# One more buffer for raw weights and for low halves, a byte mask for the scans, and reloads of gates, o, x and p at other products, in a fused short-convolution and gated-recurrence layer

## The chip, the core and the metric

The kernel runs on one core of one Trainium2 chip. The metric is the device time of one execution in microseconds (us). The core's engines appear in the profile as PE (TensorE's matmuls), PEld (its weight loads), DVE (VectorE), ACT (ScalarE), POOL (GpSimd) and SP (SyncE, here only an issuer of DMAs). DMAs are issued from two queues that matter here: SP's, which carries the weights, and POOL's, which carries activations to and from DRAM. Both are moved by the same 16 DMA engines.

## The reference, cut to what matters

One encoder layer on 2048 prompt tokens and 64 sample tokens, all in float32, with D_MODEL = 1024 and eight heads of 128:

```python
h = rms_norm(x, g_pre)
proj = jnp.einsum('btd,dn->btn', h, w_in)                 # 10 groups of 1024 columns
vA, bA, cA, zA, q, f, iv, zB, gA, gB = split_cols(proj)
u = cA * vA                                               # path a: a convolution over 3 tokens
yA = jnp.einsum('btc,cd->btd', jax.nn.silu(zA) * bA * causal_conv3(u_ext, conv_w), w_a_out)
fg = lb + (1.0 - lb) * jax.nn.sigmoid(f)                  # path b: a recurrence, head by head
S_new, o = hgrn2_scan(S0, silu(q) * QK_SCALE, 1.0 - fg, iv, jnp.log(fg))   # chunks of 64 tokens
o = o * lax.rsqrt(jnp.mean(o * o, axis=-1, keepdims=True) + EPS) * g_onorm
yB = jnp.einsum('btc,cd->btd', o * jax.nn.silu(zB), w_b_out)
merged = jax.nn.sigmoid(gA) * yA + jax.nn.sigmoid(gB) * yB
x = x + rms_norm(jnp.einsum('btd,de->bte', merged, w_o), g_post)
gate = jax.nn.sigmoid(jnp.einsum('btd,de->bte', rms_norm(x, g_ple), w_ple_gate))
x = x + jnp.einsum('btp,pd->btd', p, w_ple_proj) * gate
```

## The kernel before

**Blocks and halves.** The 2112 tokens are cut into three blocks of 768, 704 and 640 tokens. Activations lie with features on partitions; a tile of one feature block and all tokens of a block is an `r` tile (a ring of 50 of them), and a matmul takes half of the tokens: 384, 352 or 320 columns. To keep float32 accuracy with TensorE's fast form of it, each operand is split into a high half `hi` and a low half `lo`, and each product is three matmuls: hi by hi, hi by low activations, low weights by hi. The two lines of `split` (196) do it: ScalarE writes hi, VectorE subtracts it.

**Products.** The matrix products use a Strassen-like scheme with seven products instead of eight. A weight matrix is cut into 2 x 2 parts, and the parts or sums of parts (A11, A12, A22, S1 to S4) are the weights. A product here means the matmuls of one weight block of 128 x 512: 4 slices of K by 3, so 12 matmuls. A block's raw weights come by `load_raw` (line 206, 256 KB, tag `raw`, five buffers). For some, the low half is split on the spot into a `lo` tile; for the others it was stored in DRAM earlier (`low`) and is loaded again (line 228, 256 KB). `low_tile` says where a loaded low half goes: to tag `s` (three buffers) in turns 1, 3 and 5 of seven, else to `lo` (four buffers). `s` also holds the sums that the first block makes. There are five `hi` buffers. A DMA into a buffer can start when the last reader of the tile that had it before is done, and SP issues its DMAs strictly in order.

**Stages.** For each block: path b with the heads (and the gates' products between them, spilled to DRAM, line 777), path a (`path_a`), and then `in_turn` over three or four weight matrices: W_A (w_a_out), W_G (w_ple_gate, in the middle block only, and there for the rows of block 0), W_B (w_b_out), W_O (w_o). In `in_turn` each matrix has seven products n = 0 to 6 (A11, A12, S2, S3, A22, S1, S4), each for four g. So the products of a stage are numbered n x 4 + g: 20 is (W_A, n = 5, g = 0), 28 is (W_B, n = 0, g = 0). After these, the gates of the next block start (`gates`, by `sgroup`), and the norms of this block run between their first products.

**What is reloaded, and when.** `loads` is called after every product. The dict `plan` says which spilled tiles POOL reloads at which (matrix, n): gates GA and GB, o (the heads' outputs), h2 (block 0's normed rows for W_G). Such a reload is *paced*: it waits for the last matmul issued. `fetch` reloads the halves of x and p that W_G's sinks add (line 1163, two DMAs of 192 KB). `operands_in_steps` makes the operands of the next block, one step at each product in `STEPS_AT`; some steps load a pair of x (line 645, not paced). In the middle block products from 28 on are shifted by 28, since W_G stands between. `final_norm` loads x_fm (line 1205) for its residual: four at its start (three in the last block) and one with each j after that. POOL, too, issues in order.

**The scans.** `keep` is a mask of ones with a zero at each chunk's start; `tensor_tensor_scan` in `head_prep` (line 867) multiplies its running sum by it, once for each head and block.

Of the kernel before, what the change touches and what calls it, by code (L numbers as in the profile page):

```python
# [10 lines left out]
F32 = mybir.dt.float32  # L11
F32R = mybir.dt.float32r
I32 = mybir.dt.int32
AF = mybir.ActivationFunctionType
ALU = mybir.AluOpType
PSUM = bass.MemoryType.PSUM
# [25 lines left out]
LEAD = 7  # L42


STEPS_AT = (0, 8, 9, 10, 12, 13, 14, 15, 20)
STEPS_AT += (36, 37, 40, 41, 42, 43, 49, 53)
STEPS_AT += (57, 58, 65, 67, 68, 69, 70, 76)
STEPS_AT += (80, 81, 82, 83)


def plan():
# [37 lines left out]
def hybrid_step(  # L89
# [31 lines left out]
    def nm(s):  # L121
        uid[0] += 1
        return f"{s}_{uid[0]}"
# [27 lines left out]
    g_pre, g_on, g_post, g_ple = (vec[:, i, :] for i in range(4))  # L151
    cw = [vec[:, 4 + i, :] for i in range(3)]
    caus = const.tile([P, 2, P], I32, tag="caus", name="caus")
    keep = const.tile([P, MAXN], F32, tag="keep", name="keep")
    atts = [
        const.tile([P, max(len(b["parts"][i]) for b in blocks if i < len(b["parts"])), P], F32, tag=f"att{i}", name=f"att{i}") for i in range(NPART)
    ]
# [44 lines left out]


    def load_raw(src):
        raw = wp.tile([P, 4, P], F32, tag="raw", name=nm("raw"), bufs=5)
        SP.dma_start(raw, src)
        return raw

# [2 lines left out]
    def lo_tile():  # L211
        return wp.tile([P, 4, P], F32R, tag="lo", name=nm("lo"))

    def low_tile():

        turn[0] += 1
        return sum_tile(F32R) if turn[0] % 7 in (1, 3, 5) else lo_tile()

    def sum_tile(dt=F32):
        return wp.tile([P, 4, P], dt, tag="s", name=nm("s"), bufs=3)  # L220

    def split_w(raw, key=None, queue=SP, low=low_tile):

# [71 lines left out]
    def kept_w(i1, i2, name, anew=False, low=low_tile):  # L295

        keys = dict(A11=(i1, 0), A12=(i1, 1), A22=(i2, 1))
        if name in keys:
            return split_w(load_raw(w_blk[keys[name]]), None if anew else keys[name])
        return split_w(load_raw(sums[i1][name]), (i1, name), low=low)  # L300

    def combined(i1, i2, first):

        queue = SP if first else G
        with tc.high_priority():
            if not first and i1 in sums:
                lows_in = dict(S3=partial(sum_tile, F32R), S1=partial(sum_tile, F32R), S2=partial(sum_tile, F32R), S4=lo_tile)
                return {n: kept_w(i1, i2, n, True, lows_in.get(n)) for _, n, _, _, _ in PRODUCTS}
            a11, a21, a22, a12 = (load_raw(w_blk[i, h]) for i, h in ((i1, 0), (i2, 0), (i2, 1), (i1, 1)))
            out = dict(A11=split_w(a11))  # L310

            def total(name, x, y, op):
                s = sum_tile()
                V.tensor_tensor(s, x, y, op)
                out[name] = keep_sum(name, i1, s, queue) if first else split_w(s)
                return s

            total("S3", a11, a21, ALU.subtract)
            s1 = total("S1", a21, a22, ALU.add)
            s2 = total("S2", s1, a11, ALU.subtract)  # L320
            out["A12"] = split_w(a12)
            out["A22"] = split_w(a22)
            total("S4", a12, s2, ALU.subtract)
            return out
# [91 lines left out]
    def half(t, h):  # L416
        n = wide(t) // 2
        return t[:, h * n : (h + 1) * n]
# [207 lines left out]
    def rms(acc, out, segs, copy=A.copy):  # L626


        cols = col_rstds([acc[:, cols_of(sg)] for sg in segs], segs[0]["n"])
        yield  # L630
        for sg, col in zip(segs, cols):
            copy(out[:, cols_of(sg)], spread(col, sg["n"]))
        yield
# [448 lines left out]
    def ple(bl, ph, kept, held=None, shared=False):  # L1082


        for j in range(KB):
            if held is not None:
                hi, lo = held[j]
            else:
                raw = wp.tile([P, 4, P], F32, tag="raw", name=nm("raw"), bufs=5)[:, :2, :]
                SP.dma_start(raw, w_ple[j])  # L1090
                with tc.high_priority():
                    hi = wp.tile([P, 4, P], F32R, tag="hi", name=nm("hi"), bufs=5)[:, :2, :]
                    lo = low_tile()[:, :2, :]
                    A.copy(hi, raw)
                    SP.dma_start(lo.bitcast(F32), lows["p", j])
            t = rt(bl["n"])
            for s in bl["segs"]:
                pp, c = ps_attn()[:, : s["n"]], cols_of(s)
                for k, (xhi, xlo) in enumerate(ph):
                    T.matmul(pp, hi[:, k, :], xhi[:, c], start=k == 0, stop=False)  # L1100
                    T.matmul(pp, hi[:, k, :], xlo[:, c], start=False, stop=False)
                    last[0] = T.matmul(pp, lo[:, k, :], xhi[:, c], start=False, stop=k == 1).ins
                with tc.high_priority():
                    if shared and j < 4 and s is bl["segs"][1]:
                        V.tensor_copy(t[:, c], pp)
                    else:
                        copied = copies[0] = A.copy(t[:, c], pp).ins
            if bl["last"]:
                kept["p", j] = t
            else:  # L1110
                kept["p", j] = spill("p", j, wide(t))
                G.dma_start(kept["p", j], t)
                if not shared:
                    lows["p", j] = dram.tile([P, 2, P], F32, tag=f"lop{j}", name=nm("low"), bufs=1)
                    SP.dma_start(lows["p", j], lo.bitcast(F32))
            with behind_all((copied,) if hooks else ()):
                hook()
            yield
# [9 lines left out]
    def merge_in_turn(a, kept, mg, before):  # L1128

        ob, m = [], []  # L1130

        def gated(v, x, y):
            V.tensor_tensor(v, whole(x, y), v, ALU.mult)

        def sink_a(g, c, h, x, y):
            gated(half(m[g + c * KH], h), x, y)

        def sink_b(g, c, h, x, y):
            j = g + c * KH
            gated(half(mg[j], h), x, y)  # L1140
            V.tensor_tensor(half(mg[j], h), half(mg[j], h), half(m[j], h), ALU.add)

        plan = {
            (W_A, -1): (kept, GA, m),
            (W_A, 1): (kept, GA, m),
            (W_B, 1): (kept, GB, mg),
        }
        stages = [
            dict(idx=W_A, raw=a, sink=sink_a, anew=("A11", "A12")),
            dict(idx=W_B, raw=ob, sink=sink_b, anew=("A11", "A12")),  # L1150
        ]
        if before is None:
            plan |= {(W_A, 3): (kept, "o", ob), (W_A, 5): (kept, "o", ob), (W_A, 6): (kept, GB, mg)}
        else:
            rows, fetched = [], {}
            stages.insert(1, gate_in_turn(before[0], rows, lambda j, h: fetched.pop((j, h)), ("A11", "A12", "A22")))
            plan |= {(W_A, 3): (before[1], "h2", rows), (W_A, 5): (before[1], "h2", rows)}
            plan |= {(W_G, 1): (kept, "o", ob), (W_G, 2): (kept, "o", ob), (W_G, 6): (kept, GB, mg)}

        def fetch(j, h):  # L1160
            t = rt(before[0]["n"])
            for q, kind in enumerate("xp"):
                paced(G.dma_start(half(t, q), half(before[1][kind, j], h)))
            fetched[j, h] = half(t, 0), half(t, 1)

        def loads(idx, n, g=0, count=1):

            src, kind, tiles = plan.get((idx, n), (kept, None, m))
            if kind is not None:
                tiles.extend(reload(src[kind, j], n >= 0) for j in range(len(tiles), len(tiles) + count))  # L1170
            if idx == W_G and n in (0, 3, 4, 5):
                fetch(g + KH * (n in (3, 4)), int(n > 3))

        return stages, loads

# [17 lines left out]
    def final_norm(bl, segs, xo, acc, h2, kept, raw=False):  # L1193
# [10 lines left out]
                xks.append(rt(bl["n"]))  # L1204
                G.dma_start(xks[j][:, c], x_fm[j * P : (j + 1) * P, segs[0]["t0"] : segs[0]["t0"] + n])

        for _ in range(3 if bl["last"] else 4):
            fetch()
        copy = V.tensor_copy if bl["last"] else A.copy
        yield from rms(acc, rs, segs, copy)  # L1210
        for j in range(KB):
            fetch()
            xj = xo[j][:, c]
# [177 lines left out]
    for bi, bl in enumerate(blocks):  # L1391
# [14 lines left out]
        def side(rows, sums_):  # L1406
            for j in range(KB):
# [6 lines left out]
                    hooks.extend(partial(piece, sums_) if n in at else None for n in range(12))  # L1414
                yield

        def ready():
            a_first.extend(narrow(half(t, 0)) for t in a[:KH])

        path_a(bl, hc, a, first, side(rows, prepare_sums(in_path) if in_path else None), ready)  # L1420
        assert not hooks and (extra is None or next(extra, extra) is extra)
        mg, xo, h2, acc = [], [], [], []
        stages, loads = merge_in_turn(a, kept, mg, (blocks[0], kepts[0]) if middle else None)
        stages.append(out_in_turn(mg, xo, acc, ("A11", "A12", "A22") if bl["last"] else ()))
        if nxt:
            hc = new_operands()
# [5 lines left out]
        else:  # L1432
            rows2 = []
            again = rows_again(kepts[bi - 1], rows2)
        loads(W_A, -1, count=KH)
        for idx, n, g in in_turn(stages, a_first):
            loads(idx, n, g)
            if nxt:
# [75 lines left out]
```

## Time and profile before

| | |
|---|---|
| three runs, us | 2562.08, 2572.47, 2572.30 (median 2572.3) |
| the profiled execution's own time, us | 2571.89 |
| its span, first to last instruction, us | 2570.1 |
| granted TensorE clock, mean | 0.997 |
| DMA, mean over the span | 270 GB/s, 693.53 MB |

The profile's page has the span in 40 slices of 64 us, each digit a busy share in tenths:

```profile
PE   8999999999999999999999999999999999999999
DVE  8788888899989866677755577986566665568966
ACT  6666676554555666777845466666677754456736
POOL 1022121222110021223221013102100010011221
DMA  7677777898798797777777689989866667789977
```

A row of the waits is: engine, line, tile, what it waited for, us in total, times, the longest. A row of the windows is: start and end, length, then for each engine the busy time and the number of instructions, then granted clock, share of the DMA engines, GB/s. A row of the timeline is: start, length, engine, line, operation, out<-in, and in brackets the idle time before it with what ended it. In names, `raw`, `lo`, `s` and `hi` are tiles in the core's memory; `low`, `S` and `w_blk` are in DRAM.

### The profile page before, as it was taken

The page shows a single profiled execution, that of the slowest core. Times are in us where ns is not written, and L with a number is a line of the kernel's source. Part 1 is how long each engine was busy: PE and PEld are TensorE (multiplying, and loading weights), DVE is VectorE, ACT ScalarE, POOL GpSimd, SP SyncE. Part 2 cuts the span into 40 slices and gives each one's busy share as a digit, 9 for nine tenths or more (in the row PEclk, how much of TensorE's full clock was granted, in tenths as well). Part 3 has the DMA queues.
Part 4 walks back from the last instruction along what each step waited for, and adds up shares of the span by engine and source line. Part 5 has one row for each costly group of instructions (what it writes and reads, how often), then busy time and mean ns, then how long its engine had stood idle before and what let it go on. Part 6 is the DMA issues. An engine that isn't in the chain of part 4 may idle for free. (4 is left out here: it accounts for less than half of the span.)

```text
span 2570.1 us, 47304 instructions
## 1 busy us (share of the span) xinstructions
PE 2540.2 (99%) x16198; PEld 2525.4 (98%) x16198; DVE 1915.8 (75%) x3714; ACT 1617.3 (63%) x3136; POOL 421.0 (16%) x774
## 2 busy tenths in 40 slices
PE   8999999999999999999999999999999999999999
PEld 8999999999999999999999999999999999999998
DVE  8788888899989866677755577986566665568966
ACT  6666676554555666777845466666677754456736
POOL 1022121222110021223221013102100010011221
PEclk9999999999999999999999999999999999999999
DMA  7677777898798797777777689989866667789977
GB/s 269 211 262 276 275 249 265 295 317 304 264 323 265 243 342 259 257 261 267 253 263 231 215 304 358 331 276 330 308 202 198 196 207 236 233 281 337 312 263 256
DMA packets 330289, 693.53 MB, mean 270 GB/s; under 512 B 41632, under 2 KB 46272, under 8 KB 330048
## 3 DMA queue, kind: packets, MB, share of 16 engines
q1 hardware_dynamic: 283392, 513.73, 60.0%
q0 software_dynamic: 46368, 176.74, 19.0%
q8 instruction: 127, 2.08, 0.3%
q14 instruction: 114, 0.93, 0.1%
q10 hardware_dynamic: 288, 0.05, 0.0%
HBM read 507.10 MB, written 183.26 MB: 269 GB/s over the span
## 5 line engine op out<-in xcount | busy, mean ns | idle before, releaser
L385 PE MATMUL pg<-r,hi 128*128 128x320 f32 (+2 forms) x3304 | 1087.1, 329 | 0.0
L386 PE MATMUL pg<-r,hi 128*128 128x320 f32 (+2 forms) x3304 | 1067.8, 323 | 0.0
L387 PE MATMUL pg<-r,lo 128*128 128x384 f32 (+2 forms) x2368 | 771.6, 326 | 1.9 <-DMA lo<-low 1.9
L385 PEld LDWEIGHTS pg<-r,hi 128*128 128x128 f32 x3304 | 622.5, 188 | 0.4
L386 PEld LDWEIGHTS pg<-r,hi 128*128 128x128 f32 x3304 | 622.8, 188 | 0.0
L227 ACT CAST hi<-raw 128x512 fp32r<-128x512 f32 x544 | 335.2, 619 | 335.6 <-PE pg L386 131.6
L196 ACT CAST hi<-raw 128x512 fp32r<-128x512 f32 x454 | 280.9, 620 | 290.0 <-PE pg L386 133.4
L387 PEld LDWEIGHTS pg<-r,lo 128*128 128x128 f32 x2368 | 445.4, 188 | 2.4 <-DMA lo<-low 2.2
L196 DVE TENSOR_TENSOR lo<-raw,hi 128x512 fp32r<-128x512 f32 x454 | 311.6, 687 | 154.8 <-ACT hi L196 134.2
L520 PE MATMUL pg<-r,hi 128*128 128x384 f32 (+2 forms) x1232 | 398.7, 325 | 0.9 <-DVE r L196 0.7
L519 PE MATMUL pg<-r,hi 128*128 128x384 f32 (+2 forms) x1232 | 389.3, 326 | 0.4 <-ACT r L196 0.2
L387 PE MATMUL pg<-r,s 128*128 128x320 f32 (+1 forms) x936 | 296.6, 317 | 6.5 <-DMA s<-low 6.5
L196 DVE TENSOR_TENSOR r<-r,r 128x320 fp32r<-128x320 f32 (+6 forms) x426 | 245.9, 595 | 68.1 <-ACT r L196 66.1
L521 PE MATMUL pg<-r,lo 128*128 128x384 f32 (+2 forms) x860 | 278.5, 325 | 7.3 <-DMA lo<-low 7.3
L520 PEld LDWEIGHTS pg<-r,hi 128*128 128x128 f32 x1232 | 232.4, 189 | 4.6 <-DVE r L196 3.7
L196 ACT CAST r<-r 128x320 fp32r<-128x320 f32 (+6 forms) x426 | 221.0, 548 | 24.9 <-DVE r L366 16.2
L519 PEld LDWEIGHTS pg<-r,hi 128*128 128x128 f32 x1232 | 229.6, 189 | 4.9 <-ACT r L196 4.3
L387 PEld LDWEIGHTS pg<-r,s 128*128 128x128 f32 x936 | 176.8, 189 | 7.1 <-DMA s<-low 7.1
L196 ACT CAST hi<-s 128x512 fp32r<-128x512 f32 x160 | 98.7, 618 | 117.1 <-PE pg L386 104.0
L521 PEld LDWEIGHTS pg<-r,lo 128*128 128x128 f32 x860 | 161.9, 188 | 8.9 <-DMA lo<-low 8.9
L399 ACT COPY hf<-pg 128x352 f32<-128x352 f32 (+2 forms) x354 | 156.0, 444 | 10.4 <-PE pg L387 10.2
L432 DVE TENSOR_TENSOR r<-hf,pg 128x352 f32<-128x352 f32 (+2 forms) x118 | 60.9, 516 | 97.6 <-PE pg L387 97.6
(370 smaller groups left out, 3767.5 us busy)
## 6 DMA issues: line engine op xcount, KB each, us to landing
raw<-w_blk SPq DMA_DIRECT2D x550, 256.0 KB, 4.1
raw<-S SPq DMA_DIRECT2D x488, 256.0 KB, 3.8
s<-low SPq DMA_DIRECT2D x334, 256.0 KB, 4.0
lo<-low SPq DMA_DIRECT2D x210, 256.0 KB, 4.5
low<-lo SPq DMA_DIRECT2D x178, 256.0 KB, 3.0
S<-s SPq DMA_DIRECT2D x152, 256.0 KB, 3.2
low<-r POOLq DMA_DIRECT2D x88, 256.0 KB, 4.4
r<-w_blk POOLq DMA_DIRECT2D x72, 256.0 KB, 6.6
```

What stands on the lines that cost most here:

```text
L196: return A.copy(hi, src).ins, V.tensor_tensor(lo, src, hi.bitcast(F32), ALU.subtract).ins
L227: A.copy(hi, raw)
L385: add(hi[:, k, :], xhi, start=start and k == 0, stop=False)
L386: add(hi[:, k, :], xlo, start=False, stop=False)
L387: last[0] = add(lo[:, k, :], xhi, start=False, stop=k == KH - 1).ins
L399: copied = A.copy(got[n], ps[bank])
L432: V.tensor_tensor(dst, x, y, ALU.add)
L519: add(hi[:, k, :], xhi, start=start and k == 0, stop=False)
L520: add(hi[:, k, :], xlo, start=False, stop=False)
L521: last[0] = add(lo[:, k, :], xhi, start=False, stop=k == KH - 1).ins
```

## The change

- Raw weights have six buffers instead of five, `s` four instead of three. Loaded low halves go to `s` and `lo` by turns; in the groups whose sums are stored already (`combined`), S4's goes to `s` too, as those of S1, S2 and S3 did.
- `keep` is a tile of bytes, 768 bytes on each partition instead of 3072.
- In `STEPS_AT`, product 20 becomes 28: the load of the second pair of x for the next block's operands.
- In the middle block, o is reloaded at (W_A, 4) and (W_A, 6) instead of (W_G, 1) and (W_G, 2), and the 16 fetches of x and p stand at the products of `FETCH_AT` instead of all products of n = 0, 3, 4, 5.
- The first four gates GA are asked for ahead of path a's last group (`ready`), not behind it.
- `final_norm` asks for one x at its start and one after each of its steps, where it asked for four (three) together.

```diff
+FETCH_AT = (0, 1, 2, 3, 8, 9, 11, 12, 13, 14, 16, 17, 18, 19, 21, 22)
-STEPS_AT = (0, 8, 9, 10, 12, 13, 14, 15, 20)
+STEPS_AT = (0, 8, 9, 10, 12, 13, 14, 15, 28)
...
-    keep = const.tile([P, MAXN], F32, tag="keep", name="keep")
+    keep = const.tile([P, MAXN], KEEP, tag="keep", name="keep")
...
-        raw = wp.tile([P, 4, P], F32, tag="raw", name=nm("raw"), bufs=5)
+        raw = wp.tile([P, 4, P], F32, tag="raw", name=nm("raw"), bufs=6)
...
-        return sum_tile(F32R) if turn[0] % 7 in (1, 3, 5) else lo_tile()
+        return sum_tile(F32R) if turn[0] % 2 else lo_tile()
...
-        return wp.tile([P, 4, P], dt, tag="s", name=nm("s"), bufs=3)
+        return wp.tile([P, 4, P], dt, tag="s", name=nm("s"), bufs=4)
...
-                lows_in = dict(S3=partial(sum_tile, F32R), S1=partial(sum_tile, F32R), S2=partial(sum_tile, F32R), S4=lo_tile)
-                return {n: kept_w(i1, i2, n, True, lows_in.get(n)) for _, n, _, _, _ in PRODUCTS}
+                return {n: kept_w(i1, i2, n, True, partial(sum_tile, F32R)) for _, n, _, _, _ in PRODUCTS}
...
-            plan |= {(W_G, 1): (kept, "o", ob), (W_G, 2): (kept, "o", ob), (W_G, 6): (kept, GB, mg)}
+            plan |= {(W_A, 4): (kept, "o", ob), (W_A, 6): (kept, "o", ob), (W_G, 6): (kept, GB, mg)}
+            order = [(g + c * KH, h) for c, h in ((0, 0), (1, 0), (1, 1), (0, 1)) for g in range(KH)]
...
-            if idx == W_G and n in (0, 3, 4, 5):
-                fetch(g + KH * (n in (3, 4)), int(n > 3))
+            if idx == W_G and order and n * KH + g in FETCH_AT:
+                fetch(*order.pop(0))
...
-        for _ in range(3 if bl["last"] else 4):
-            fetch()
-        copy = V.tensor_copy if bl["last"] else A.copy
-        yield from rms(acc, rs, segs, copy)
+        fetch()
+        copy = V.tensor_copy if bl["last"] else A.copy
+        for _ in rms(acc, rs, segs, copy):
+            fetch()
+            yield
...
         def ready():
             a_first.extend(narrow(half(t, 0)) for t in a[:KH])
+            loads(W_A, -1, count=KH)
...
-        loads(W_A, -1, count=KH)
```

Lines of the changed kernel are three or four higher than those of the one before (206 is 210, 228 is 232, 234 is 238, 1123 is 1126, 1205 is 1206).

**SP's queue in block 0, W_A, ahead of S1's products.** Rows are in the order of issue; `S_959_3846` and `w_blk` are raw weights in DRAM, `low_1874`, `low_3190` and `low_2135` the stored low halves of S1's g = 0, S1's g = 2 and S4's g = 0; an L234 or L238 row stores the low half of an A22 that was split on the spot. Before:

```order
L206 DMA raw_9450<-S_959_3846 128x512
L234 DMA low_9310<-lo_9307 128x512
L206 DMA raw_9480<-S_524_2133 128x512
L228 DMA s_9535<-low_3451 128x512
L206 DMA raw_9506<-S_693_2791 128x512
L234 DMA low_9336<-lo_9333 128x512
L228 DMA lo_9359<-low_1874 128x512
L206 DMA raw_9532<-S_862_3449 128x512
L228 DMA lo_9423<-low_3190 128x512
```

After, from four rows ahead of the first store:

```order
L232 DMA s_9359<-low_1874 128x512
L210 DMA raw_9330<-w_blk 128x512
L210 DMA raw_9356<-S_452_1872 128x512
L232 DMA s_9419<-low_3190 128x512
L210 DMA raw_9386<-S_621_2530 128x512
L210 DMA raw_9416<-S_790_3188 128x512
L232 DMA s_9479<-low_2135 128x512
L238 DMA low_9258<-lo_9255 128x512
L210 DMA raw_9446<-S_959_3846 128x512
L238 DMA low_9284<-lo_9281 128x512
```

`low_1874` stood behind all four stores of A22 and went to a `lo` tile; now it stands ahead of them and goes to an `s` tile (row 522 of SP's, where it was row 536).

**POOL's queue in block 1, W_A, from n = 3 on.** `h` is block 0's normed rows, `o` the heads' outputs. Before:

```order
L1123 DMA r_19267<-h_3029_12223 128x768
L645 DMA r_19393<-x_fm 128x640
L645 DMA r_19395<-x_fm 128x640
L1123 DMA r_19397<-h_3035_12258 128x768
L1123 DMA r_19427<-h_3038_12277 128x768
L1123 DMA r_19457<-h_3041_12299 128x768
L1123 DMA r_19487<-h_3045_12320 128x768
L1163 DMA r_19609<-x_12065 128x384
```

After:

```order
L1126 DMA r_19267<-h_3029_12223 128x768
L1126 DMA r_19293<-o_13274 128x704
L1126 DMA r_19319<-o_13743 128x704
L1126 DMA r_19345<-o_14217 128x704
L1126 DMA r_19371<-o_14693 128x704
L1126 DMA r_19401<-h_3035_12258 128x768
L1126 DMA r_19431<-h_3038_12277 128x768
L1126 DMA r_19461<-h_3041_12299 128x768
L1126 DMA r_19491<-h_3045_12320 128x768
L1126 DMA r_19517<-o_15177 128x704
L1126 DMA r_19543<-o_15661 128x704
```

The eight o stand among h2's rows and behind them, and no longer in W_G; the pair of x_fm is gone from here, to W_B.

**POOL's queue where the gates of block 1 and the norm of block 0 begin.** L581 (L584) is the power that makes 1/sqrt of the norm; L777 (L780) spills a gate. Before:

```order
L1205 DMA r_11221<-x_fm 128x768
L1205 DMA r_11223<-x_fm 128x768
L1205 DMA r_11225<-x_fm 128x768
L1205 DMA r_11227<-x_fm 128x768
L581 TENSOR_TENSOR colsum_11229<-colsum_11229,mhalf 128x6
L1205 DMA r_11362<-x_fm 128x768
```

After:

```order
L1206 DMA r_11221<-x_fm 128x768
L1206 DMA r_11236<-x_fm 128x768
L584 TENSOR_TENSOR colsum_11223<-colsum_11223,mhalf 128x6
L1206 DMA r_11280<-x_fm 128x768
L780 DMA g__2808_11299<-r_11119 128x704
L1206 DMA r_11360<-x_fm 128x768
```

Two of the four x_fm ahead of the power have moved behind it.

More of the change, by code (lines that the diff above doesn't have):

```diff
@@ L13 @@
 I32 = mybir.dt.int32
+KEEP = mybir.dt.uint8
 AF = mybir.ActivationFunctionType
@@ L1088, in ple @@
             else:
-                raw = wp.tile([P, 4, P], F32, tag="raw", name=nm("raw"), bufs=5)[:, :2, :]
+                raw = wp.tile([P, 4, P], F32, tag="raw", name=nm("raw"), bufs=6)[:, :2, :]
                 SP.dma_start(raw, w_ple[j])
@@ L1141, in sink_b @@
             V.tensor_tensor(half(mg[j], h), half(mg[j], h), half(m[j], h), ALU.add)
[L1143 to L1147, printed above, removed]
         stages = [
@@ L1151, in merge_in_turn @@
         ]
+        plan = {(W_A, -1): (kept, GA, m), (W_A, 1): (kept, GA, m), (W_A, 6): (kept, GB, mg), (W_B, 1): (kept, GB, mg)}
         if before is None:
-            plan |= {(W_A, 3): (kept, "o", ob), (W_A, 5): (kept, "o", ob), (W_A, 6): (kept, GB, mg)}
+            plan |= {(W_A, 3): (kept, "o", ob), (W_A, 5): (kept, "o", ob)}
+            order = []
         else:
@@ L1415, in side @@
                 yield
+        mg, xo, h2, acc = [], [], [], []
+        stages, loads = merge_in_turn(a, kept, mg, (blocks[0], kepts[0]) if middle else None)
         def ready():
             a_first.extend(narrow(half(t, 0)) for t in a[:KH])
+            loads(W_A, -1, count=KH)
         path_a(bl, hc, a, first, side(rows, prepare_sums(in_path) if in_path else None), ready)
         assert not hooks and (extra is None or next(extra, extra) is extra)
-        mg, xo, h2, acc = [], [], [], []
-        stages, loads = merge_in_turn(a, kept, mg, (blocks[0], kepts[0]) if middle else None)
         stages.append(out_in_turn(mg, xo, acc, ("A11", "A12", "A22") if bl["last"] else ()))
```

## The prediction

> **What bounds the kernel now.** I read the page first.
>
> ```profile
> span 2570.1 us, 47304 instructions
> PE 2540.2 (99%) x16198; PEld 2525.4 (98%) x16198; DVE 1915.8 (75%) x3714; ACT 1617.3 (63%) x3136; POOL 421.0 (16%) x774
> ```
>
> TensorE is busy 2540.2 of 2570.1 us, and the change takes no matmul away: its 16,198 matmuls stand in nearly the same order after it. So nothing can be won but TensorE's idle time, 29.9 us, and whatever makes matmuls slow. The second view is the waits, for TensorE alone.
>
> ```profile
> PE pg L521 <- DMA lo<-low: 7.3, 5, 3.0
> PE pa L1100 <- ACT r L196: 6.8, 1, 6.8
> PE pg L387 <- DMA s<-low: 6.5, 2, 3.5
> PE pg L387 <- DMA lo<-low: 1.9, 1, 1.9
> PE pg L520 <- DVE r L196: 0.7, 1, 0.7
> ```
>
> (microseconds in total, times, longest.) 6.8 us is the start, before the first operand; the change doesn't touch it. Three rows name one thing, a low half of a weight that had not landed: 7.3 + 6.5 + 1.9 = **15.7 us** in eight waits. What is left of the idle time is the end of the kernel (TensorE's last matmul comes some 6 us before it). The third view is windows; the column after the five engines is the clock granted to TensorE.
>
> ```profile
> 746.80:750.10 3.30, 3.30 (x12) 3.30 (x11) 0.21 (x1) 1.24 (x3) 0.54 (x1) 0.50 0.62 228
> 890.10:893.40 3.30, 3.30 (x11) 3.30 (x12) 0.34 (x1) 0.00 (x0) 0.00 (x0) 0.50 0.19 71
> 1600.10:1603.40 3.30, 3.30 (x12) 3.30 (x12) 1.66 (x5) 1.41 (x3) 1.52 (x4) 0.50 1.06 398
> 1733.20:1736.50 3.30, 3.30 (x15) 3.30 (x14) 0.00 (x0) 0.00 (x0) 0.00 (x0) 0.50 0.01 4
> ```
>
> Behind four of the waits TensorE runs 3.3 us at half clock. Half of 3.3 is lost: 4 x 1.65 = **6.6 us**, which counts as busy on the page. So late low halves cost 15.7 + 6.6 = 22.3 us, 0.9% of the time; that is all this change can win.
>
> [...]
>
> **Why the halves are late.** Two waits, with the DMA that each is for:
>
> ```profile
> 736.97 0.32 SPq L228 DMA_DIRECT2D lo<-low  x1
> ...
> 746.05 0.44 PE L521 MATMUL pg<-r,lo 128*128 128x384 f32 x1 [2.47 <-DMA lo<-low]
> ...
> 882.79 0.32 SPq L228 DMA_DIRECT2D s<-low  x1
> ...
> 890.10 0.66 PE L387 MATMUL pg<-r,s 128*128 128x352 f32 x1 [3.48 <-DMA s<-low]
> ```
>
> (start, length.) 9.1 us pass from issue to use in the first and 7.3 in the second, where the median landing is 4:
>
> ```profile
> s<-low SPq DMA_DIRECT2D x334, 256.0 KB, 4.0
> lo<-low SPq DMA_DIRECT2D x210, 256.0 KB, 4.5
> ```
>
> Just ahead of each, POOL issued large transfers together:
>
> ```profile
> 735.15 0.54 POOL L1123 DMA_DIRECT2D r<-o  x1 [1.33 <-PE pg L521]
> 735.69 1.07 POOL L645 DMA_DIRECT2D r<-x_fm  x2
> ...
> 880.77 0.54 POOL L1205 DMA_DIRECT2D r<-x_fm  x1 [12.52 <-DVE r L432]
> 881.63 0.54 POOL L1205 DMA_DIRECT2D r<-x_fm  x1 [0.33 <-DVE r L695]
> 882.56 0.54 POOL L1205 DMA_DIRECT2D r<-x_fm  x1 [0.40 <-DVE r L432]
> 883.83 0.54 POOL L1205 DMA_DIRECT2D r<-x_fm  x1 [0.73 <-ACT hi L227]
> ```
>
> The third long wait, in block 1's gate stage, has reloads of o before it, four within 3 us, and then halves of x and p behind each other:
>
> ```profile
> 1576.47 1.06 POOL L1123 DMA_DIRECT2D r<-o  x2 [1.30 <-ACT hi L227]
> 1577.79 0.54 POOL L1123 DMA_DIRECT2D r<-o  x1 [0.26 <-ACT hi L227]
> 1579.27 0.54 POOL L1123 DMA_DIRECT2D r<-o  x1 [0.95 <-ACT hi L196]
> 1581.36 0.54 POOL L1163 DMA_DIRECT2D r<-x  x1 [1.55 <-ACT hi L196]
> 1581.89 0.54 POOL L1163 DMA_DIRECT2D r<-p  x1
> ...
> 1598.94 0.44 PE L521 MATMUL pg<-r,lo 128*128 128x384 f32 x1 [3.03 <-DMA lo<-low]
> ```
>
> The windows of that block (last columns: share of the DMA engines, GB/s) show how full they are:
>
> ```profile
> 1516.00:1552.00 36.00, 36.00 (x227) 36.00 (x225) 28.47 (x59) 23.55 (x49) 5.36 (x10) 1.00 1.03 385
> 1552.00:1564.00 12.00, 12.00 (x71) 11.76 (x70) 11.94 (x25) 6.26 (x13) 4.26 (x8) 1.00 0.79 245
> 1564.00:1612.00 48.00, 44.97 (x246) 44.11 (x245) 34.41 (x70) 29.92 (x61) 22.44 (x42) 0.96 1.03 384
> ```
>
> About 385 GB/s is what they move when full. 227 matmuls in 36.0 us make 1.90 us for a product (12 matmuls), in which SP wants a raw block and a low half, 2 x 262 KB: 276 GB/s. One POOL reload of 352 to 384 KB per product makes that 465.
>
> The fourth long wait, near 1728, is the second's twin, one block later. So a low half is late where a burst of POOL's meets a short lead. The lead is read from the order: a load can go out once the product that last used its buffer has ended. A22's products split their lows on the spot and take all four lo; the next lo waits for the first of them, three products back, 3 x 1.9 to 2.1 = about 6 us. That is under the 9.1 that the first wait needed.
>
> **The change part by part.** *Buffers.* With lows alternately in s and lo, four each, the first of S1 comes from s: its load stands 14 rows earlier in SP's queue, and its lead is eleven products instead of three. The short lead passes to the next one, as four. Followed through the program's waits, 53 of the 552 loaded halves have a lead of four products or less before, and 17 after (nine have three); the usual six becomes seven in `in_turn`. In the first groups of the next block, where the waits at 890 and 1728 lie, the late s has six instead of four, 4 us more against 3.5 missing. The sixth raw buffer lets raw blocks go out one product earlier. Cost: none on an engine; SP issues the same DMAs.
>
> *x_fm of the operands from product 20 to 28.* POOL reaches it 12 products later, behind the gates' reloads, where A11 and A12 of w_b_out load no lows. Two transfers of 352 KB leave the first burst; they are first used at product 36, over 15 us later. *Norms.* Two x_fm at the first step instead of four, then one at a step: same bytes, and each x is then asked for three steps ahead of its use, not four (in the last block three already). *o, x, p.* In block 1 o moves from the gate stage to w_a_out, and x and p go out up to four products earlier. These edits take the burst from all four long waits. *Gates at the path's end.* POOL already ran ahead to them in blocks 1 and 2; in block 0 they pass the two stores of one sum of w_o, which is read two stages later: 0.
>
> *The mask in bytes* is read by the scans:
>
> ```profile
> L867 DVE TENSOR_TENSOR_SCAN r<-keep,r 128x768 f32<-128x768 f32 x8 | 14.0, 1750 | 0.8 <-ACT r L865 0.8
> L867 DVE TENSOR_TENSOR_SCAN r<-keep,r 128x704 f32<-128x704 f32 x8 | 12.9, 1616 | 2.2 <-ACT r L865 2.2
> L867 DVE TENSOR_TENSOR_SCAN r<-keep,r 128x640 f32<-128x640 f32 x8 | 11.9, 1482 | 2.0 <-ACT r L865 2.0
> ```
>
> No scan with bytes is in the trace. Bounds: half to double of 38.8 us over 24 heads, so -0.8 to +1.6 us of VectorE per head. VectorE is idle for 25% of the span and no wait of TensorE's names a scan; I take 0 for TensorE, and the cover ends when a head has under 1.6 us of VectorE left.
>
> *Sum.* The profiled execution took 2571.9 us, 1.8 over its span and 0.4 under the median of 2572.3. 2571.9 - 15.7 - 6.6 = 2549.6 with no late half at all. What stays: of the eight waits, five fell on the 22 halves with a lead of three or less and three on the 31 with four. At those rates nine and eight halves would give 9 x 5/22 + 8 x 3/31 = 2.8 waits, each 15.7/8 + 6.6/8 = 2.8 us: 7.8 us. But the bursts behind the long ones are gone, so between 0 and 7.8 I take the middle, 3.9: **2553.5 us**.
>
> **Rivals.** *A new wait in w_a_out of block 1.* It gains eight o (2.9 MB) and loses two x_fm of 320 KB, 2.2 MB more in a stretch that runs at 385 already: 5.8 us of DMA time. The lead of seven products, 13.3 us, leaves 4.2 over the slowest landing above (9.1), so 1.6 us could be missing, and with one drop of the clock 1.65 more: 2553.5 + 3.3 = 2557. Against it, the next 12 us run at 245 and have room.
>
> *The waits stay.* The full DMA engines, not bursts or leads, are the cause; lows that go out earlier also land later. Half of the 22.3 us then stays, 2561, or all, 2572. For it: of the three runs before one took 2562.08, so such waits come and go by themselves. Against it: 7.3 and 9.1 us of landing stand beside a median of 4.
>
> *Slower.* The leads don't help, and POOL's 16 reloads in a row in w_a_out of block 1 starve SP: one per 1.90 us takes about 190 of 385 GB/s, SP keeps 195, and a product takes 524 KB / 195 = 2.69 us instead of 1.90. 16 x 0.79 = 12.6 us, with four drops of the clock 6.6 more; only the gate stage's 4.7 goes: 2571.9 + 12.6 + 6.6 - 4.7 = 2586. It decides once landings there pass 13.3 us.
>
> [...]
>
> **How the numbers follow.** Forecast (2549 to 2558) 0.65, new wait in w_a_out (2555 to 2561) 0.12, waits stay (2560 to 2574) 0.19, slower (2585 and more) 0.04. A measurement of this kernel tells about 0.5% from no change, 12.9 us: faster is below 2559.4. The first case and nearly all of the second lie there, with a little of the third: 0.77 faster, 0.19 the same, 0.04 slower. The range runs from the floor of 2549 into the waits that stay, to 2566.
>
> **What would show it.** Right: in TensorE's waits the rows on lo and s shrink from 15.7 to under 4 us, no window but the start and end has a clock of 0.50, and POOL's rows before 743, 886 and 1728 no longer stand in bunches. New wait: a row on lo in the products S3 to S4 of block 1's w_a_out. Mask wrong: the L867 row's mean, and a wait of TensorE's on the heads' r. The forecast falls if the rows on late halves still hold over 10 us.

## The result, and the profile after

| | before | after |
|---|---|---|
| median, us (lowest to highest, runs) | 2571.86 (2562.08 to 2576.23, 6) | 2553.12 (2550.53 to 2555.44, 6) |
| ratio, 95% interval | | 0.9933 (0.9915 to 0.9951) |
| the profiled execution, us | 2571.89 | 2552.61 |
| its span, us | 2570.1 | 2550.6 |

The change makes the kernel faster: 0.67% by the ratio of the runs, 18.7 us between the two medians. The page of after, with the same two lines as before:

```profile
span 2550.6 us, 47470 instructions
PE 2534.3 (99%) x16198; PEld 2519.8 (99%) x16198; DVE 1915.9 (75%) x3714; ACT 1618.7 (63%) x3136; POOL 421.3 (17%) x774
```

The span is 19.5 us shorter. TensorE's busy time fell by 5.9 us with the same number of matmuls, and its idle time from 29.9 to 16.3. VectorE, ScalarE and POOL did the same work in the same busy time. TensorE's waits after, the four largest (us in total, times, longest):

```profile
PE pa L1103 <- ACT r L200: 6.9, 1, 6.9
PE pg L522 <- ACT r L200: 1.1, 1, 1.1
PE pg L524 <- DMA lo<-low: 0.9, 1, 0.9
PE pg L523 <- DVE r L200: 0.6, 1, 0.6
```

Of 15.7 us for late low halves 0.9 is left, in one wait. The rows with `r` at L522 and L523 are waits for an operand, split from activations; they grew from 0.9 (0.7 and 0.2) to 1.7. The 0.6 lie near 1555, where the gate stage of block 1 begins, and the 1.1 near 1613, behind that stage, in w_b_out. The fall of the idle time, 13.6, is 14.8 less these 0.8, a new wait of 0.3 near 64 us and 0.1 at the start. Windows of after at the places of the four long waits (last three columns: granted clock, DMA share, GB/s):

```profile
743.00:748.00 5.00, 5.00 (x31) 5.00 (x30) 3.05 (x7) 2.81 (x7) 1.07 (x2) 1.00 0.90 311
886.00:891.00 5.00, 5.00 (x35) 4.98 (x34) 3.78 (x8) 4.18 (x9) 1.38 (x1) 1.00 0.67 196
1595.00:1600.00 5.00, 4.98 (x29) 4.66 (x28) 5.00 (x11) 2.31 (x6) 1.82 (x4) 1.00 1.04 390
1726.00:1731.00 5.00, 5.00 (x38) 4.99 (x37) 2.56 (x5) 3.45 (x8) 3.22 (x5) 1.00 0.98 348
...
1510.00:1546.00 36.00, 36.00 (x224) 36.00 (x223) 28.51 (x60) 22.39 (x46) 8.79 (x17) 1.00 1.03 388
1546.00:1558.00 12.00, 11.37 (x65) 10.77 (x64) 9.61 (x20) 8.28 (x16) 4.06 (x8) 1.00 1.04 382
1558.00:1606.00 48.00, 47.98 (x273) 46.92 (x272) 41.20 (x83) 32.23 (x68) 21.97 (x41) 1.00 0.97 349
```

TensorE is busy through all four at full clock: the 0.50 is gone. In block 1 the moved o now stand in the 36 us of w_a_out's end, which were full before and still are, and in the 12 us behind them, which go from 245 to 382 GB/s; the 48 us of the gate stage fall from 384 to 349. POOL's queue at the first two places:

```profile
734.46 0.54 POOL L1126 DMA_DIRECT2D r<-o  x1 [1.31 <-PE pg L524]
745.29 0.54 POOL L1126 DMA_DIRECT2D r<-o  x1 [10.30 <-ACT hi L231]
...
875.39 0.54 POOL L1206 DMA_DIRECT2D r<-x_fm  x1 [12.55 <-DVE r L435]
876.26 0.54 POOL L1206 DMA_DIRECT2D r<-x_fm  x1 [0.33 <-DVE r L698]
889.62 1.56 POOL L584 TENSOR_TENSOR colsum<-colsum,mhalf 128x6 f32<-128x6 f32 x1 [12.83 <-DVE colsum L582]
891.15 0.59 POOL L1206 DMA_DIRECT2D r<-x_fm  x1
```

The pair of x_fm behind the o at 735 is gone, and two of the four x_fm at 880 now come behind the power.

### The profile page after: what moved, and what is told of

Its sections match the earlier page's. It is cut to its first block, busy times and chain, and to the rows that moved or that the text cites. A ratio compares the mean times of both kernels' runs of the same rounds, so it can differ in the third digit from the quotient of the medians.

```text
span 2550.6 us, 47470 instructions
## 1 busy us (share of the span) xinstructions
PE 2534.3 (99%) x16198; PEld 2519.8 (99%) x16198; DVE 1915.9 (75%) x3714; ACT 1618.7 (63%) x3136; POOL 421.3 (17%) x774
## 5 line engine op out<-in xcount | busy, mean ns | idle before, releaser
L390 PE MATMUL pg<-r,lo 128*128 128x384 f32 (+2 forms) x2056 | 673.0, 327 | 0.0
L523 PE MATMUL pg<-r,hi 128*128 128x384 f32 (+2 forms) x1232 | 398.1, 325 | 1.1 <-DVE r L200 0.6
L390 PE MATMUL pg<-r,s 128*128 128x320 f32 (+1 forms) x1248 | 393.9, 316 | 0.1
L522 PE MATMUL pg<-r,hi 128*128 128x384 f32 (+2 forms) x1232 | 388.2, 325 | 1.1 <-ACT r L200 1.1
L390 PEld LDWEIGHTS pg<-r,lo 128*128 128x128 f32 x2056 | 386.2, 188 | 0.0
L524 PE MATMUL pg<-r,lo 128*128 128x384 f32 (+2 forms) x800 | 257.8, 324 | 0.9 <-DMA lo<-low 0.9
L523 PEld LDWEIGHTS pg<-r,hi 128*128 128x128 f32 x1232 | 231.3, 188 | 5.9 <-DVE r L200 4.7
L390 PEld LDWEIGHTS pg<-r,s 128*128 128x128 f32 x1248 | 234.4, 188 | 0.3 <-DMA s<-low 0.3
L522 PEld LDWEIGHTS pg<-r,hi 128*128 128x128 f32 x1232 | 228.5, 188 | 5.7 <-ACT r L200 5.0
L402 ACT COPY hf<-pg 128x352 f32<-128x352 f32 (+2 forms) x354 | 156.0, 444 | 10.5 <-PE pg L390 10.3
L524 PEld LDWEIGHTS pg<-r,lo 128*128 128x128 f32 x800 | 150.2, 188 | 1.6 <-DMA lo<-low 1.5
L524 PE MATMUL pg<-r,s 128*128 128x320 f32 (+2 forms) x432 | 139.1, 322 | 0.0
```

Source lines behind the costliest of these rows:

```text
L390: last[0] = add(lo[:, k, :], xhi, start=False, stop=k == KH - 1).ins
L402: copied = A.copy(got[n], ps[bank])
L522: add(hi[:, k, :], xhi, start=start and k == 0, stop=False)
L523: add(hi[:, k, :], xlo, start=False, stop=False)
L524: last[0] = add(lo[:, k, :], xhi, start=False, stop=k == KH - 1).ins
```

## The experiments

The kernels were measured in three lots, each with its own runs of the kernel before (medians 2570.61, 2571.04 and 2571.56). All compute the whole result. The first lot takes the change apart into buffers and places. All with a change in the number of buffers carry the mask in bytes too, which frees 2304 bytes on each partition.

**The buffers alone**, with S4's low half in `s` as in the change:

```diff
-        raw = wp.tile([P, 4, P], F32, tag="raw", name=nm("raw"), bufs=5)
+        raw = wp.tile([P, 4, P], F32, tag="raw", name=nm("raw"), bufs=6)
...
-        return sum_tile(F32R) if turn[0] % 7 in (1, 3, 5) else lo_tile()
+        return sum_tile(F32R) if turn[0] % 2 else lo_tile()
...
-        return wp.tile([P, 4, P], dt, tag="s", name=nm("s"), bufs=3)
+        return wp.tile([P, 4, P], dt, tag="s", name=nm("s"), bufs=4)
```

> The buffers alone (six raw, four s, lows by turns, byte mask), every reload where it was. Theory (a late low half needs a burst of POOL's and a short lead; longer leads help at the four long sites): the leads there go from 3 or 4 products to 6 to 11, so the waits of 2.5, 3.5, 3.0 and 3.1 us and their clock drops go, but the bursts stay and the halves that now have the short lead can be late: waits on low halves 2 to 7 us in all, at most one clock drop, 2553 to 2561. Rival 'bursts alone': leads do nothing, waits on low halves stay at 12 to 18 us, 2568 to 2575. Rival 'leads alone': as the whole change, under 2 us of waits, 2551 to 2555.

Measured: 2550.86 us, ratio 0.9921 (0.9907 to 0.9936). So the buffers bring all of the gain, with every burst of POOL's where it was. Its waits on low halves:

```profile
PE pg L521 <- DMA lo<-low: 2.4, 2, 2.2
```

The waits near 890 and 1728 are gone and that near 746 is down to 0.2, though their bursts stayed; the one near 1590 is left with 2.2. The theory that both the burst and the short lead must go had this kernel at 2553 to 2561 with 2 to 7 us of waits; the rival, by which longer leads are enough, had 2551 to 2555 with under 2 us. The time is the rival's (0.1 us under its range), and of the four long waits it explains three; the 2.4 us of waits are just what the theory allowed.

**The places alone**: all of the change but the buffers (`STEPS_AT`, `FETCH_AT`, o, GA and the norms; raw 5, s 3, the old turns, and the mask in float32 as before).

```diff
-STEPS_AT = (0, 8, 9, 10, 12, 13, 14, 15, 20)
+STEPS_AT = (0, 8, 9, 10, 12, 13, 14, 15, 28)
...
-            plan |= {(W_G, 1): (kept, "o", ob), (W_G, 2): (kept, "o", ob), (W_G, 6): (kept, GB, mg)}
+            plan |= {(W_A, 4): (kept, "o", ob), (W_A, 6): (kept, "o", ob), (W_G, 6): (kept, GB, mg)}
```

> The reloads of gates, o, x and p and the norms' x at their new places, with the old buffers (five raw, three s, the old turns of lows, float mask). Theory: the bursts at 743, 886 and 1728 are smaller, but the short leads stay (3 at product 20 of w_a_out, 4 in the next block's first groups): waits on low halves 3 to 9 us, 2555 to 2563; w_a_out of block 1, where o now comes, may show a wait of 1 to 3 us, since leads are six there. Rival 'bursts alone': under 2 us of waits, 2551 to 2555. Rival 'leads alone': 12 to 18 us of waits, 2568 to 2575.

Measured: 2560.77 us, 0.9961 (0.9947 to 0.9975), about half the gain. Its waits:

```profile
PE pg L524 <- DVE r L200: 3.9, 7, 1.1
PE pg L391 <- DMA s<-low: 1.8, 2, 1.1
PE pg L525 <- DMA lo<-low: 1.3, 3, 0.6
PE pg L523 <- ACT r L200: 1.1, 1, 1.1
PE pg L391 <- DMA lo<-low: 0.7, 1, 0.7
```

Without the bursts the low halves are late six times still, 3.8 us together, but by 1.1 us at most, and no stretch of that kernel between its start and its end has half clock. The two `r` rows, operands split too late, have grown from 0.9 to 5.0 us in eight waits. Two of these, 1.8 us at 1548 and 1550, stand just behind the moved o, where after has one of 0.6; ahead of them ScalarE's cast of a raw block at 1545.08 had waited 1.84 us for its DMA. Two, 1.1 us near 1500, stand ahead of the moved o and are not its doing: waits of 0.4 to 0.7 near there are also in the kernel before, in the norms alone, in the mask alone and in the low halves' buffers alone, all with five raw buffers, and in no kernel with six. One of 1.1 lies in block 0, near 771.

**The norms alone**: the loop that asks for x_fm after each step, and nothing else.

```diff
-        for _ in range(3 if bl["last"] else 4):
-            fetch()
+        fetch()
...
+        for _ in rms(acc, rs, segs, copy):
+            fetch()
+            yield
```

> Only the norms ask for x singly. Theory: of the eight waits on low halves the two of 3.5 and 3.1 us near 886 and 1728 go or shrink under 1 us, with both clock drops (1.7 us each): about 9 us, 2561 to 2565; the waits near 743 and 1596 stay. Rival 'leads alone': nothing, 2568 to 2575, both waits stay over 2 us.

Measured: 2564.46 us, 0.9976 (0.9965 to 0.9987), inside the theory's range, with 6.2 us where it had about 9. The wait of 3.5 us near 890 fell to 0.9 and its twin of 3.1 near 1728 to 0.3, both without a drop of the clock; those near 746 and 1595 stayed at 2.7 and 3.5 us. One trace alone would not show it, since these waits vary from one execution to the next (near 1728 the kernel with the mask alone has 1.4 us and no drop); the runs' ratio does. So the bunch of four x_fm was a cause of the two waits, and longer leads a second cure for the same ones: the two gains do not add.

**The mask alone**: `keep` in bytes.

```diff
-    keep = const.tile([P, MAXN], F32, tag="keep", name="keep")
+    keep = const.tile([P, MAXN], KEEP, tag="keep", name="keep")
```

> Only the scans' mask in bytes. Theory: the scans take the same 1.48 to 1.75 us within 2%, the time stays at 2568 to 2575. Rival 'bytes are slower (or faster) to read': the scans' mean moves by over 10%; doubled it is 38 us more of VectorE, and TensorE waits for operands of the heads.

Measured: 2570.57 us, 1.0000 (0.9989 to 1.0010): nothing. A group's row in its profile has the scan's mean at the same 1750 ns as before:

```profile
L868 DVE TENSOR_TENSOR_SCAN r<-keep,r 128x768 f32<-128x768 uint8 x8 | 14.0, 1750 | 0.8 <-ACT r L866 0.8
```

The scans of 704 and 640 tokens kept their means as well, 1616 and 1482 ns, here and in the profile of after, to 1 ns.

The second lot asks whether the places add anything to the buffers, and which buffer it is. **The whole change again**, beside **the buffers again**:

> The whole change, beside the buffers alone on the same chip. Theory now (leads first; the new places add little on top of them): within 0.2% of the buffers alone, 2550 to 2555. Rival 'the moved o costs': 2 us or more above the buffers alone, from waits on operands (r) in w_a_out and the gate stage of block 1. Rival 'the places still help': 2 us or more below.

> The buffers alone once more, for the comparison with the whole change on one chip: 2550 to 2554 by every theory; one wait of 2 to 3 us near 1590, where the gate stage's reloads still come together, is expected again by the theory that a burst still matters where the lead is four.

Measured: 2551.21 us, 0.9928 (0.9914 to 0.9943), and 2552.25 us, 0.9931 (0.9917 to 0.9945). The two can't be told apart. What differs is the place of the one wait on a low half that is left: 1.5 us near 1624 in the whole, 3.2 us near 1591 in the buffers alone. The latter's timeline, and a window behind it:

```profile
1591.36 0.69 PE L521 MATMUL pg<-r,lo 128*128 128x384 f32 x1 [3.24 <-DMA lo<-low]
```

```profile
1591.40:1598.20 6.80, 6.80 (x24) 6.80 (x25) 2.43 (x5) 1.94 (x5) 1.08 (x2) 0.57 1.04 388
```

**The low halves' buffers alone** (with S4's in `s`; raw stays at five):

```diff
-        return sum_tile(F32R) if turn[0] % 7 in (1, 3, 5) else lo_tile()
+        return sum_tile(F32R) if turn[0] % 2 else lo_tile()
...
-        return wp.tile([P, 4, P], dt, tag="s", name=nm("s"), bufs=3)
+        return wp.tile([P, 4, P], dt, tag="s", name=nm("s"), bufs=4)
```

> Four s buffers and lows by turns, five raw buffers as before, reloads as before. Theory 'the lead of the low half': all of the buffers' gain, 2550 to 2556, waits on low halves under 5 us, no or one clock drop. Rival 'raw blocks behind': SP reaches a low only after the raw in front of it, so five raw buffers keep half of the waits, 2558 to 2566.

and **the raw buffer alone** (`s` stays at three, the turns as they were):

```diff
-        raw = wp.tile([P, 4, P], F32, tag="raw", name=nm("raw"), bufs=5)
+        raw = wp.tile([P, 4, P], F32, tag="raw", name=nm("raw"), bufs=6)
```

> Six raw buffers, lows as before, reloads as before. Theory 'the lead of the low half': leads of lows stay at three and four, so the waits stay: 2567 to 2574 and 11 to 18 us of waits on low halves. Rival 'raw blocks behind': half or more of the gain, 2553 to 2563.

Measured: 2554.23 us, 0.9937 (0.9922 to 0.9953), and 2572.17 us, 1.0001 (0.9988 to 1.0014). The raw buffer by itself brings nothing; its low halves are as late as ever, 18.4 us in the profiled execution, which took 2575.79 us (in the mask alone, with the same leads, 11.7 us in one of 2566.14):

```profile
PE pg L522 <- DMA lo<-low: 11.0, 6, 5.2
...
PE pg L388 <- DMA s<-low: 5.5, 2, 3.0
PE pg L388 <- DMA lo<-low: 1.9, 1, 1.9
```

The low halves' buffers bring nearly all, 16.8 us of the 18.8 that the buffers bring in this lot. (The edit holds a fourth `s` and new turns; a fourth `s` with the old turns was not run.) What they lack shows as 3.1 us of waits for operands, 2.9 of them on VectorE. Ahead of the longest, 1.4 us that end at 1601.1, ScalarE's timeline in that kernel has

```profile
1594.10 0.62 ACT L228 CAST hi<-raw 128x512 fp32r<-128x512 f32 x1 [0.93 <-DMA raw<-S]
...
1597.16 0.62 ACT L197 CAST hi<-raw 128x512 fp32r<-128x512 f32 x1 [1.24 <-DMA raw<-w_blk]
```

and VectorE's

```profile
1597.82 0.69 DVE L197 TENSOR_TENSOR lo<-raw,hi 128x512 fp32r<-128x512 f32 x1 [0.72 <-ACT hi L197]
...
1600.50 0.99 DVE L197 TENSOR_TENSOR r<-r,r 128x384 fp32r<-128x384 f32 x2
```

The cast of a raw block waits for its DMA, VectorE's half of the split waits for the cast, and after four steps of the sinks come the operands that TensorE waits for. In both timelines the work for the operand stands behind these waits, so a late raw block becomes a late operand. With the sixth buffer the two executions of the buffers alone have 0.3 us or less of these. In time the 2 us are only hinted at, since the intervals overlap.

The third lot takes the leads by themselves. The short leads come from A22: its low halves are split on the spot and all go to `lo`, so that the next loads into `lo` wait for products just behind them. This edit gives them turns like the loaded ones; in the whole change the shortest lead becomes four products, as counted from the program (three halves have it, the others five and more):

```diff
-    def split_w(raw, key=None, queue=SP, low=low_tile):
+    def split_w(raw, key=None, queue=SP, low=low_tile, spot=lo_tile):
...
-        lo = lo_tile()
+        lo = spot()
...
-    def kept_w(i1, i2, name, anew=False, low=low_tile):
+    def kept_w(i1, i2, name, anew=False, low=low_tile, spot=lo_tile):
...
-            return split_w(load_raw(w_blk[keys[name]]), None if anew else keys[name])
+            return split_w(load_raw(w_blk[keys[name]]), None if anew else keys[name], spot=spot)
...
-                    hi, lo = kept_w(i1, i2, IN_TURN[n][0], IN_TURN[n][0] in st["anew"])
+                    hi, lo = kept_w(i1, i2, IN_TURN[n][0], IN_TURN[n][0] in st["anew"], spot=low_tile)
```

**In the whole change**, and **in the buffers alone**:

> The whole change, and in in_turn the halves that are split on the spot also take s and lo by turns, so that every loaded half there has a lead of five to seven products (the shortest three or four of the whole change go, but for three halves with four). Theory 'leads first': the wait near 1612 to 1625 (0.9 to 1.5 us) goes, 2549.5 to 2552, waits on low halves under 0.5 us. Rival 'full DMA engines': that wait stays, no difference from the whole change.

> The same turns on top of the buffers alone, reloads where they were. Theory 'leads first': the wait of 2 to 3 us near 1590 goes (lead four becomes six), 2549.5 to 2552, as the whole change with these turns. Rival 'bursts still count': the burst of o, x and p in the gate stage makes landings of 10 to 12 us there, so a wait of 1 to 3 us stays near 1590 to 1600: 2551 to 2555.

Measured: 2548.96 us, 0.9908 (0.9895 to 0.9922; runs from 2547.10 to 2549.54), the lowest median here; and 2551.74 us, 0.9921 (0.9907 to 0.9934; runs from 2551.03 to 2552.54). The first is 0.5 us below what was expected; it was measured in another lot than the whole change, and their intervals overlap, so that it is the faster of the two is not shown. Its rows on late halves are down to 0.3 us and those on operands in and behind the gate stage to 0.5. In the second no low half is late any more, as the theory had it, but operands are, where the rival had its wait:

```profile
PE pg L520 <- DVE r L197: 2.0, 2, 1.8
PE pg L519 <- ACT r L197: 1.3, 1, 1.3
```

Here the places do count, by 2.8 us: all runs of the one are under all runs of the other. DMAs issued from 1575 to 1602 us, in the gate stage of block 1 (times, KB each, median us from issue to landing), with the new places:

```profile
r<-x POOLq DMA_DIRECT2D x7, 192.0 KB, 5.8
...
raw<-S SPq DMA_DIRECT2D x5, 256.0 KB, 7.6
lo<-low SPq DMA_DIRECT2D x4, 256.0 KB, 9.0
```

and with the old ones:

```profile
r<-x POOLq DMA_DIRECT2D x10, 192.0 KB, 5.7
...
lo<-low SPq DMA_DIRECT2D x4, 256.0 KB, 12.5
raw<-S SPq DMA_DIRECT2D x3, 256.0 KB, 12.6
```

With more of x and p at that time, 20 loads and not 14, SP's loads from `low` and `S` landed later by 2.6 to 5.0 us at the median (those from `w_blk` in 10.7 in both), while POOL's of x and p landed in 5.7 to 6.2 in both. The even leads still cover it for low halves; the raw blocks no longer come in time, and operands wait behind them. ScalarE's waits for DMAs in these 27 us are, with the old places,

```profile
ACT hi L228 <- DMA raw<-S: 5.0, 3, 2.1
ACT hi L197 <- DMA raw<-w_blk: 0.6, 1, 0.6
```

and with the new ones there is none.

**The buffers with the norms and the later step** (product 28), but o, x, p and GA at the old places:

```diff
-STEPS_AT = (0, 8, 9, 10, 12, 13, 14, 15, 20)
+STEPS_AT = (0, 8, 9, 10, 12, 13, 14, 15, 28)
...
-        for _ in range(3 if bl["last"] else 4):
-            fetch()
+        fetch()
...
+        for _ in rms(acc, rs, segs, copy):
+            fetch()
+            yield
```

> The buffers, the norms' x singly and the operands' x at product 28, but o, x and p of the gate stage and the gates at the path's end as before. Theory: the wait of 2 to 3 us near 1590 stays and the one near 1624 doesn't come; 2551 to 2554, no different in time from the buffers alone or the whole. Rival 'the norm and the steps still help': 2 us or more below the buffers alone.

Measured: 2552.23 us, 0.9923 (0.9909 to 0.9936), no different from the buffers alone. A wait of 2.9 us near 1590 and one of 1.5 near 1627 are in its trace. The second was not expected: I had put the wait near 1624 down to the moved o, and it is here without that.

**The edit for even leads alone**, on the kernel before with its buffers, turns and places:

> The kernel before with one edit: in in_turn the halves split on the spot take s and lo by the old turns of seven too. Three s, five raw, old places. Leads of three and four become five and six at the sites near 743, 843, 1596 and 2350, and five (from four) near 886 and 1728; the one near 1746 keeps three. Theory 'the lead, not the number of buffers': waits on low halves fall from 16 to 3 to 7 us, 2553 to 2560. Rival 'the added buffers are what helps': 2566 to 2574.

Measured: 2555.78 us, 0.9935 (0.9922 to 0.9949). No buffer more and no reload moved, and 15.8 of the 18.7 and 19.8 us that the whole change brought are there. Low halves are late by 2.2 us in all, less than the 3 to 7 expected. The first site shows how: ahead of product 20, SP's loads of low halves go out at 732.2, 733.8, 735.0 and 736.2 us, where before they went out at 734.9, 737.0, 739.1 and 741.2. Those to `lo` land no sooner (a median of 9.3 us from 733 to 747, before 7.9), and the wait is 0.3 us instead of 2.5. So which earlier product a load has to wait for is the main cause, not the number of buffers.

## Why the prediction was right

The forecast was 2553.5 us and the median is 2553.12. Point by point:

- **What was at stake.** Right. 15.7 us of waits and 6.6 of half clock were named as all there was to win; waits on low halves fell by 14.8, and TensorE's busy time by 5.9, where 6.6 of half clock were to go.
- **What stays.** The term of 3.9 us came out as 3.0 in the profiled execution (2552.6 against the floor of 2549.6), for a reason that was half wrong. It was meant for late halves; they hold 0.9 us there (1.5 in the other trace of the same kernel). Of the rest, 0.8 are waits for operands (1.7 against 0.9 before), which the prediction didn't name, 0.4 a new wait near 64 us and a longer start, and 0.7 what TensorE's busy time fell short of the 6.6. The longer of the operands' waits, 1.07 us at 1613.29, comes from a late raw block, as in the kernel with the low halves' buffers alone; ScalarE's rows in the changed kernel:

```profile
1611.88 0.62 ACT L200 CAST hi<-raw 128x512 fp32r<-128x512 f32 x1 [1.83 <-DMA raw<-w_blk]
...
1612.75 0.49 ACT L200 CAST r<-r 128x352 fp32r<-128x352 f32 x1
```

The cast of the operand stands behind one that waited for its raw block. Ahead of the other, 0.6 us at 1554.86, VectorE had been busy without a break since 1547.75; what began that is not shown. And 3.9 was the middle of 0 to 7.8, at one average price for a wait with its drop of the clock, where the traces have waits of like length with and without one (below). So the 0.4 us between forecast and median are luck: single runs of the kernel lie 4.9 us apart.
- **Norms.** Right, and shown alone: near 890 and 1728 the waits shrink to 0.9 and 0.3 us and their drops go.
- **Buffers.** The direction was right and the weight wrong. "A low half is late where a burst of POOL's meets a short lead" holds in so far as removing either is enough where it is removed. But the prediction let the buffers and the moves each do a part of the work, and the runs show that longer leads do all of it, the places half, the raw buffer by itself none. The parts don't add: 19.8 us and 9.8 us make 18.7 in one measurement of the whole and 19.8 in the other.
- **"These edits take the burst from all four long waits."** Right for three, shown alone for the two of the norms. The stretch with the fourth, near 1599, fell from 384 to 349 GB/s. The one late half that is left comes behind it, near 1625 in w_b_out.
- **The mask.** Right: the scan's mean didn't move, and the kernel with it alone is the kernel before.
- **The rivals.** *A new wait in w_a_out of block 1*: not in the changed kernel, where those 36 us have no idle time, and the DMAs were as full as computed (388 GB/s). With the old buffers 1.8 us of operand waits stand behind the moved o, about what the rival had without its drop of the clock; so the place was nearly right and the tile wrong, and with the new buffers 0.6 us are left of it. *The waits stay* and *slower* fell; the slower one had SP down to 195 GB/s and needed landings over 13.3 us. In those 36 us of the changed kernel SP's queue moved 8.5 MB, 236 GB/s (259 before), its loads landed in medians of 5.3 to 10.3 us, and TensorE lost nothing there.

What is open in part: where the wait near 1624 comes from. Its low half has one of the short leads left, of three products, and the even leads took it away, which speaks for the lead. That lead is in the buffers alone too, where no half is late there. The four loads to `lo` between 1613 and 1626 landed in a median of 5.9 and 6.8 us in the two traces of the buffers alone, without a wait; in 7.1 and 7.7 us in the two of the whole change and 7.6 with the norms and the later step, with waits of 0.9, 1.5 and 1.5 us. So this too looks like a short lead that meets slow landings; what slows them there was not tried.

## What to carry to other kernels

When a load into a rotating buffer is late, look first at which earlier reader it waits for: a class of tiles that takes its turns from one pool only gave leads of three products beside a usual six, and spreading the turns brought four fifths of the gain without a byte of memory. Count a burst on one queue and a short lead on another as one cause with two cures, and don't add their gains. When the loads that are named are cured, look for the next late ones on the same queue under another name: here they were operands behind a cast that waited 1.83 us for its raw block.

## What the runs showed of the hardware

**In these runs the length of a wait did not tell whether the clock falls behind it.** In one execution, that of the raw buffer alone, a wait of 2.96 us left the granted clock at 1.00, and one of 1.85 us, 15 us later, was followed by half clock:

```profile
1733.28 0.42 PE L388 MATMUL pg<-r,s 128*128 128x320 f32 x1 [2.96 <-DMA s<-low]
1748.37 0.42 PE L388 MATMUL pg<-r,lo 128*128 128x320 f32 x1 [1.85 <-DMA lo<-low]
```

```profile
1733.20:1736.50 3.30, 3.22 (x22) 3.22 (x23) 0.77 (x2) 0.00 (x0) 0.00 (x0) 1.00 0.16 58
1748.90:1752.20 3.30, 3.30 (x14) 3.30 (x13) 1.03 (x2) 1.29 (x3) 0.00 (x0) 0.51 0.91 359
```

The number of matmuls in the two windows, 22 and 14, says the same. The other traces have both kinds too: a wait of 1.91 us in the kernel before (at 1748.51) and one of 2.24 us in the buffers alone (at 1590.14) had no drop behind them, one of 1.78 us in the raw buffer alone (at 2352.70) had one. With even leads on the old kernel three waits of 0.40, 0.76 and 1.20 us within 4 us had a drop behind them:

```profile
1593.14 0.44 PE L521 MATMUL pg<-r,lo 128*128 128x384 f32 x1 [0.40 <-DMA lo<-low]
1595.04 0.44 PE L520 MATMUL pg<-r,hi 128*128 128x384 f32 x1 [0.76 <-DVE r L196]
1596.86 0.62 PE L519 MATMUL pg<-r,hi 128*128 128x384 f32 x2 [1.20 <-ACT r L196]
```

```profile
1599.00:1600.00 1.00, 1.00 (x5) 1.00 (x4) 1.00 (x4) 0.00 (x0) 0.00 (x0) 0.50 1.05 409
```

What decides it is not shown here, so a price of 1.65 us for the drop behind one wait is an average. The stretch behind the wait of 3.24 us above was twice as long as the 3.3 us of the four in the kernel before: 0.57 over 6.8 us, 2.9 us of work lost.

**With the DMA engines full from 1575 to 1602, the two queues moved about the same and waited unequally.** In that stretch of the two kernels with even leads, at 388 and 389 GB/s, POOL's queue moved 5.2 MB with the new places and 5.7 with the old ones, SP's 5.3 and 4.8. Yet POOL's loads of x and p, 192 KB each, landed in medians of 5.7 to 6.2 us and SP's of 256 KB in 7.6 to 12.6. SP's loads from `low` and `S` took longer where POOL had more to move, but the landings alone don't show in what order the engines took the two queues' packets, nor how long a transfer stood behind others of its own queue.
